# One forget-bias tile per head, a re-priced task order, and three PSUM banks for scores beside two for projections

## The chip, the core and the metric

The kernel runs on one core of a Trainium2 chip. The metric is the time of one execution in device microseconds (us); lower is better. Engines are named as the profile names them: PE (TensorE matmul) with PEld (its weight loads), DVE (VectorE), ACT (ScalarE), POOL (GpSimd), SP (SyncE, which issues the DMAs). Each engine runs its own list of instructions in order, and waits at an instruction whose inputs or buffers are not there.

## The reference

One layer of a hybrid attention encoder over two requests that share weights: a prompt of 1040 rows (16 meta tokens and 1024 frames) and a sample of 32 rows with a cache of 272 rows. The input is normalised, projected, and split into a differential attention group (4 heads of two maps, bias by distance, mask by chunks of 64) and a forgetting attention group (8 heads of 64, causal). The forgetting group's bias is the part that the change touches:

```python
logf = jax.nn.log_sigmoid((fl + b_f_l).astype(jnp.float32))
F = jnp.cumsum(LF, axis=1)
...
sf = jnp.einsum('bqhe,bkhe->bhqk', qf, Kf).astype(f32) * scale
sf = sf + (Fq_t[:, :, :, None] - Fk_t[:, :, None, :])
sf = jnp.where(kidx[None, :] <= qidx[:, None], sf, NEG)
pf = jax.nn.softmax(sf, axis=-1)
of = jnp.einsum('bhqk,bkhe->bqhe', pf.astype(Vf.dtype), Vf)
```

Since a softmax over k does not change when a number that depends on q alone is added, the bias of a key may be F at any reference point minus F of that key. The heads' outputs are multiplied by silu(gate), projected with w_out, added to the input and normalised:

```python
y = x + (out.astype(x.dtype) * jax.nn.silu(gate)) @ w_out_l
...
y_prompt = _rmsnorm(hp[:, N_META:], final_norm_g)
```

The new rows of k, v and log f are outputs too.

## The kernel before

The program first builds a graph of tasks, and `Graph.order` (line 149) simulates it: each task (`add`, line 100) names an engine, a cost in ns, a priority (a smaller number goes first), the tasks it depends on, the buffers it takes (`acq`) and uses (`use`). At each moment a free engine starts its ready task of smallest priority for which buffers are free. The order in which tasks start in this simulation is the order in which their instructions are written, one after the other, to every engine. So the costs are no computation of the kernel; they settle the order alone. The costs are formulas (`c_mm`, `c_act`, `c_dve`, `c_ts`, `c_pool`, lines 266 to 279, with `MARGIN` 1.1) or numbers at the place, a change of engine costs one of `HOPS` (line 33), and a DMA's landing follows from lines 203 to 209: SP is busy for `cost`, the bytes go one transfer after the other at 2.85 ns per KB, 0.9 us later they are there, and 8 may be in flight. A task of an output tile that will be ready within `AHEAD` ns holds back later ones.

Buffers come from rings (`RINGS`, line 247). The plan counts the free ones of a ring. The tile that a task gets in the program is the ring's next in turn. PSUM has 8 banks: pj 3 (projections and the output projection), sc 2 (scores, and small work of the sample), tr 1 (transposes, and the spread of a scale), av 2 (attention times values). Other memory is taken from one `arena`.

The work, in pairs p of heads or maps (p 0 to 3 differential, p 4 to 7 forgetting, two heads each):

- `x_tasks` (line 471) normalises x and writes it transposed, in f16 high and low parts, as hT.
- `w_tasks` (611) loads 128 columns of a weight, finds its largest value (ACT L627; `spread_task`, line 575: POOL L583 makes a diagonal, PE L587 spreads it into tr, DVE L600 takes the maximum) and splits it in high and low parts.
- `proj_tasks` (796) does a projection (kinds v, k, q, g for the gate) in three groups of columns, four for v and k of pair 0. Each group takes one pj bank and writes 24 matmuls (L827) in three parts of 8, between which other work may go. Its readers: for k and v ACT L845; for q ACT L889 and DVE L894, and in the last group L905 and L910; for the gate ACT L920 (exp), then DVE L924, ACT L928 and L929, DVE or POOL L933, DVE L937, and DVE L938, which reads the bank last.
- `forget_tasks` (979) computes log f and its running sum F for 8 heads. Lines 1106 to 1116 subtract F at four columns, one per group of 256 queries (DVE L1113), and store the results as four sections of `G_s`.
- `bias_tasks` (1148) makes the bias tile of 128 x 1040 in the ring G of two. For p below 4 it is made once per pair. For p of 4 and more the first call loads the pair's rows of G_s, scales them (POOL L1180) and stores them in `G_t`; every call then loads one section's first 272 + 256 gg columns, broadcast over 128 partitions (SP L1192), for one head and one group gg.
- `unit_tasks` (1206) does two blocks of 128 queries: scores (PE L1235 and, for the causal mask, L1237) in chunks of at most 512 keys, each in one sc bank; DVE L1249 adds the bias, takes the minimum and writes to the arena; ACT L1255 the exponential with its sum; DVE L1259 and L1261 the reciprocal; split in high and low f16 parts on ACT, POOL and DVE (L1284 to L1323); SP L1335 transposes by DMA; PE L1347 to L1354 multiply with the values into av. `fin_tasks` writes the result to mix_s in DRAM.
- `sample_tasks` (1448) does the same for the 32 sample rows.
- `out_tasks` (1607) splits w_out, and for nine row tiles loads mix and gate, multiplies them (L1723), finds the scale (ACT L1737 and a spread), splits (ACT L1740, DVE L1742), multiplies with w_out (L1770, two halves, each with a pj bank), adds x (L1784), squares (L1789), normalises (L1808) and stores (L1811).

`pair_tasks` (1843) calls these for a pair. For p of 4 and more its units go in the order (head 0, gg 0), (head 1, gg 0), (head 0, gg 1) and so on, eight in all, each with a bias tile of its own:

```python
for u, (hd, gg) in enumerate(units):
    if p >= 4 or u == 0:
        dist = bias_tasks(p, hd, gg, base + u - 1, G_done)
```

The projections of later pairs and the gate (priorities from 10000) fill TensorE between the units.

## Time and profile before

| | us |
|---|---|
| median of 3 runs (lowest, highest) | 882.83 (881.67, 883.38) |
| profiled execution, its time | 879.12 |
| its span, first to last instruction | 877.4 |
| mean granted clock of TensorE | 0.909 of full speed |

A row of the waits reads "engine line waited for: us in total, times, longest us"; PE av L1351 <- DMA arena<-arena is a matmul of line 1351 into av that waited for a DMA from arena to arena, here the transpose. A row of the groups of instructions reads: line, engine, operation, what it writes and reads, shapes, count, then busy us and mean ns of one, then the idle time of the engine just before them with what ended it. In the table of windows each engine has its busy us and its instructions (x), followed by the granted clock (1.00 is full), the busy share of the DMA engines and GB/s. In the timeline a row has its start and length in us; in brackets stands the idle time before it and what ended it.

### The profile page before, as it was taken

The numbers are of one execution on the slowest core, as the hardware profiler recorded it, in microseconds if no ns is written. First come the engines' busy times: TensorE is split into PE (matmuls) and PEld (weight loads), VectorE is DVE, ScalarE is ACT, GpSimd is POOL, SyncE is SP. The second block draws the span as 40 slices with busy tenths as digits, with TensorE's granted clock in tenths as the row PEclk, the third lists the DMA queues.
The fourth block names the chain that finished last, engine by engine and source line by source line (L and its number), as shares of the span: only waits on it lengthen the run. The fifth ranks groups of instructions, "written<-read, shape, count | busy, mean of one in ns | idle before, by whom it ended". The sixth has DMA issues, their size and how long they took to land. (4 is left out here: it accounts for less than half of the span.)

```text
span 877.4 us, 14974 instructions
## 1 busy us (share of the span) xinstructions
PE 703.1 (80%) x4967; PEld 456.3 (52%) x4967; DVE 633.0 (72%) x1672; ACT 496.5 (57%) x1136; POOL 414.3 (47%) x602
## 2 busy tenths in 40 slices
PE   4578887987876999899796978689788962888776
PEld 4455554665544576566564755356556542233333
DVE  5976587877766887988985857497797895454443
ACT  5843574666553776676675665377568752242222
POOL 2575233977556866866743654445452244200000
PEclk7679989999998999999998989799999985698899
DMA  8672426454423554554499688467959989753511
GB/s 248 122 147 62 93 54 88 106 94 103 95 65 74 127 102 98 115 117 115 105 194 182 127 168 163 111 144 167 208 123 204 277 204 243 232 173 121 153 63 49
DMA packets 240558, 119.27 MB, mean 136 GB/s; under 512 B 150569, under 2 KB 229745, under 8 KB 240481
## 3 DMA queue, kind: packets, MB, share of 16 engines
q1 hardware_dynamic: 240480, 118.32, 60.4%
q8 instruction: 39, 0.64, 0.3%
q14 instruction: 39, 0.31, 0.1%
HBM read 57.18 MB, written 22.07 MB: 90 GB/s over the span
## 5 line engine op out<-in xcount | busy, mean ns | idle before, releaser
L827 PE MATMUL pj<-hT,Whi 128*128 128x384 f16 (+4 forms) x1328 | 314.7, 321 | 2.0 <-DVE ge L938 1.5
L827 PE MATMUL pj<-hT,Wlo 128*128 128x416 f16 (+4 forms) x664 | 212.6, 320 | 4.4 <-DVE Wlo L648 4.4
L827 PEld LDWEIGHTS <-Whi 128*128 128x128 f16 x1328 | 133.3, 102 | 78.5 <-issue 11.5
L1249 DVE CUSTOM_DVE_ANT_0 arena<-sc,G,stats 128x400 f32<-128x400 f32 (+6 forms) x224 | 129.9, 590 | 43.3 <-PE sc L1235 22.4
L1255 ACT ACTIVATE arena<-arena,stats 128x144 f32<-128x144 f32 (+7 forms) x128 | 99.9, 780 | 38.8 <-DVE stats L1249 31.6
L1235 PE MATMUL sc<-k,q 128*128 128x400 f16 (+6 forms) x448 | 97.1, 317 | 29.4 <-DVE stats L1249 25.7
L583 POOL TENSOR_SCALAR diag<-ident,stats 128x128 bf16<-128x128 f32 x51 | 26.1, 513 | 154.9 <-ACT Wlo L1737 68.5
L827 PEld LDWEIGHTS <-Wlo 128*128 128x128 f16 x664 | 67.6, 102 | 38.1 <-DVE Wlo L648 4.7
L1351 PE MATMUL av<-arena,vn 128*128 128x128 f16 x288 | 43.9, 236 | 45.2 <-DMA arena<-arena 44.7
L1235 PEld LDWEIGHTS <-q 128*128 128x128 f16 x448 | 40.8, 101 | 57.6 <-issue 41.1
L627 ACT ACTIVATE Wlo<-raw 128x1024 bf16<-128x1024 f32 x27 | 28.5, 1055 | 63.8 <-DMA raw<-in_w_in_dram 63.8
L1770 PEld LDWEIGHTS <-Whi 128*128 128x128 f16 (+2 forms) x304 | 30.1, 102 | 58.7 <-issue 16.5
L827 PE MATMUL pj<-hT,Wghi 128*128 128x256 f16 (+2 forms) x240 | 58.2, 326 | 0.0
L1770 PE MATMUL pj<-arena,Whi 128*128 128x512 f16 (+4 forms) x152 | 49.7, 413 | 9.8 <-ACT Whi L1740 7.1
L1352 PEld LDWEIGHTS <-vn 128*128 128x128 f16 x288 | 30.7, 107 | 48.6 <-issue 47.6
L1290 POOL TENSOR_TENSOR arena<-arena 128x16 f16<-128x16 f32 (+7 forms) x56 | 46.5, 853 | 12.4 <-ACT arena L1284 12.1
L1306 DVE SCALAR_TENSOR_TENSOR arena<-arena,stats 128x128 f16<-128x128 f32 (+4 forms) x80 | 49.6, 663 | 2.6 <-ACT arena L1298 2.4
L1323 POOL TENSOR_TENSOR arena<-arena 128x16 f16<-128x16 f32 (+3 forms) x48 | 36.0, 773 | 25.8 <-ACT arena L1317 25.7
L1789 ACT ACTIVATE arena<-arena 128x512 bf16<-128x512 f32 (+3 forms) x19 | 11.5, 603 | 61.4 <-DVE arena L1784 61.4
L1352 PE MATMUL av<-arena,vn 128*128 128x128 f16 x288 | 44.3, 237 | 0.0
L1784 DVE SCALAR_TENSOR_TENSOR arena<-pj,stats,arena 128x512 f32<-128x512 f32 (+3 forms) x19 | 13.7, 721 | 42.3 <-PE pj L1770 38.9
L587 PE MATMUL tr<-diag,onesb 128*128 128x128 bf16 x51 | 11.7, 229 | 36.9 <-POOL diag L583 24.6
(310 smaller groups left out, 1786.7 us busy)
## 6 DMA issues: line engine op xcount, KB each, us to landing
raw<-in_w_in_dram SPq DMA_DIRECT2D x32, 512.0 KB, 7.5
arena<-in_x_prompt_dram SPq DMA_DIRECT2D x16, 512.0 KB, 9.7
raw<-in_w_out_dram SPq DMA_DIRECT2D x16, 512.0 KB, 4.6
k<-k SPq DMA_DIRECT2D x16, 268.0 KB, 3.4
G<-G_t SPq DMA_DIRECT2D x8, 520.0 KB, 4.7
mix_s<-mx SPq DMA_DIRECT2D x32, 128.0 KB, 3.4
arena<-mix_s SPq DMA_DIRECT2D x8, 512.0 KB, 6.3
arena<-gate_s SPq DMA_DIRECT2D x8, 512.0 KB, 6.0
```

The source lines that it names most:

```text
L583: pool.tensor_scalar(out=loc["d"], in0=ident, scalar1=col_, scalar2=1.0, op0=ALU.mult, op1=ALU.mult)
L627: ta = add("act", c_act(1024), lambda: act.activation(out=loc["lo"].bitcast(BF16), in_=loc["raw"], func=AF.Abs, accum_out=a), prio, [tl], ...
L827: mm(out, (W["hi"], W["hi"], W["lo"])[w][:, k, :], (hTh, hTl, hTh)[w][:, k, c0:c1], start=i == 0, stop=i == 23)
L1235: mm(s[:, :b - a], q, K[p]["t"][:, m, x, a:b], start=x == 0, stop=x == 1 and not mask)
L1249: dve.tensor_tensor_reduce(out=A(ph, nk)[:, a:b], in0=loc["s"][:, :b - a], in1=bl["t"][:, o + a:o + b], scale=Q[p]["tau"], scalar=3e38 if ...
L1255: te = add("act", c_act(nk) + 150, lambda ph=ph, nk=nk, mn=mn, sm=sm: act.activation(out=A(ph, nk), in_=A(ph, nk), func=AF.Exp, scale=-1.0 ...
L1290: (pool if on_pool else dve).tensor_tensor(out=A16(w, o, o + b - a), in0=x[:, a:b], in1=A16(w, h, h + b - a), op=ALU.subtract)
L1306: dve.scalar_tensor_tensor(out=A16(w, o, o + b - a), in0=x[:, a:b], scalar=rk, in1=A16(w, h, h + b - a), op0=ALU.mult, op1=ALU.subtract)
L1323: pool.tensor_tensor(out=A16(w, o, o + b - a), in0=x[:, a:b], in1=A16(w, h, h + b - a), op=ALU.subtract)
L1351: mm(out, vn[:, j, 128 * hd:128 * hd + 128], hi, start=j == 0, stop=False)
L1352: mm(out, vn[:, j, 128 * hd:128 * hd + 128], lw, start=False, stop=False)
L1770: mm(d, a, b, start=k == 0 and i == 0, stop=k == 7 and i == len(ops) - 1)
```

## The change

Three things are changed at once; the arithmetic of scores and outputs is otherwise the same.

1. One forget-bias tile per head. F is taken relative to column 528 alone; G_s and G_t have 1040 columns per head in place of 4160; a pair loads and scales two rows; a head's tile of 1040 columns is loaded once per pair and used for all four groups of queries.
2. Costs of the planner. Formulas and numbers at the place are replaced; a hop's cost depends on the producing engine; TensorE is charged twice the cost after 3.4 us of idleness, for 3.4 us; a DMA transpose (`block`) holds the DMA queue in the plan; a ring's buffers are taken in turn in the plan too, as they are in the program.
3. PSUM: pj 2 and sc 3.

In `out_tasks` a part of the matmuls names the two pieces of w_out that it reads in place of all eight.

```diff
-HOPS = [400.0, 300.0], [500.0, 300.0]
+HOPS = {"pe": 220.0, "sp": 100.0, "act": 80.0, "dve": 80.0, "pool": 80.0}
+SLACK = {"pe": 0.0, "act": 0.0, "dve": 0.0, "pool": 0.0, "sp": 0.0}
+COLD = 3400.0
+TRANSPOSED = 2000.0
+LANDED = 1600.0
...
-MARGIN = 1.1
...
-                if self.free[h.ring] < 1:
+                if self.slots[h.ring][self.turn[h.ring]]:
                     break
-                self.free[h.ring] -= 1
+                h.at = self.turn[h.ring]
+                self.slots[h.ring][h.at] = True
+                self.turn[h.ring] = (h.at + 1) % self.free[h.ring]
...
-                        busy[e] = now + t.cost
+                        cost = t.cost
+                        if e == "pe":
+                            if now > last + COLD:
+                                slow = COLD
+                            cost += min(cost, slow)
+                            slow = max(0.0, slow - cost + t.cost)
+                            last = now + cost
+                        busy[e] = now + cost
                         done = busy[e]
-                        if e == "sp":
-                            moved = max(done + 650.0, moved) + t.move
-                            done = moved + 900.0
-                            flight = (flight + [done] * t.n)[-8:]
-                            if len(flight) == 8:
-                                busy[e] = max(busy[e], flight[0])
+                        if t.dma:
+                            if t.block:
+                                busy[e] = done = moved = max(now, moved - 300.0) + t.cost
+                                done += TRANSPOSED
+                            else:
+                                busy[e] = max(busy[e], moved - 4000.0)
+                                moved = max(busy[e] + 300.0, moved) + t.move
+                                done = moved + LANDED
...
-    RINGS = {"pj": 3, "sc": 2, "tr": 1, "av": 2, "stv": 1, "raw": 2, "W": 3, "Wg": 2, "zT": 2, "stg": 2, "vn": 2, "K": 2,
+    RINGS = {"pj": 2, "sc": 3, "tr": 1, "av": 2, "stv": 1, "raw": 2, "W": 3, "Wg": 2, "zT": 2, "stg": 2, "vn": 2, "K": 2,
...
-        return k * max(107.0, 0.417 * n)
+        return k * max(56.0, 2.5 + 0.417 * n)
...
-        return MARGIN * k * (75.0 + 0.84 * n)
+        return k * (165.0 + 0.85 * n)
...
-        return MARGIN * k * (65.0 + 1.05 * n)
+        return k * (165.0 + 1.08 * n)
...
-        return MARGIN * (100.0 + 1.1 * n)
+        return 240.0 + 1.05 * n
...
-        return MARGIN * k * (100.0 + 2.2 * n)
-
-    def dma(fn, prio, deps=(), acq=(), use=(), kb=128, n=1, spare=(), cost=480.0):
-        t = add("sp", cost * n, fn, prio, deps, acq, use, 2.85 * kb, spare)
+        return k * (160.0 + 2.2 * n)
+
+    def dma(fn, prio, deps=(), acq=(), use=(), kb=128, n=1, spare=(), cost=440.0, move=4.5, block=False):
+        t = add("sp", cost * n, fn, prio, deps, acq, use, move * kb, spare)
...
-        td = add("pool", 260, fd, prio, list(deps) + [cn["id"]], [dh])
-        return loc, th, add("pe", 110, f, prio, [td, cn["one"]], [th], [dh])
+        td = add("pool", 370, fd, prio, list(deps) + [cn["id"]], [dh])
+        return loc, th, add("pe", 60, f, prio, [td, cn["one"]], [th], [dh])
...
+        def fg():
+            F = A(Fh, 1040, NH)
+            dve.tensor_scalar(out=A(gh, 1040, NH), in0=F, scalar1=F[:, 528:529], scalar2=None, op0=ALU.subtract)
+        tg = add("dve", 65 + 0.6 * 1040, fg, prio, carry, [gh], [Fh])
+        G_done["p"] = dma(lambda: sp.dma_start(out=G_s, in_=A(gh, 1040, NH)), prio, [tg], [], [gh])
...
-        n = 272 + 256 * gg
-        if ("G", p) not in samp:
+        if hd == 0:
...
+        c = 2 * (p - 4) + hd
 
         def f():
             loc["t"] = T([128, 1040], F32, "G", RINGS["G"])
-            c = 1040 * (4 * hd + gg)
-            sp.dma_start(out=loc["t"][:, :n], in_=G_t.rearrange("h n -> (h n)")[None, 8320 * (p - 4) + c:8320 * (p - 4) + c + n]
-                         .broadcast_to([128, n]))
-        cn["bias"] = dma(f, prio, [samp["G", p], cn["bias"]], [h], kb=n / 2)
+            sp.dma_start(out=loc["t"], in_=G_t[c:c + 1].broadcast_to([128, 1040]))
+        cn["bias"] = dma(f, prio, [samp["G", p], cn["bias"]], [h], kb=520)
...
-                     prio, [tl], [z], [w], kb=20 * nt, cost=1190.0)
+                     prio, [tl], [z], [w], kb=20 * nt, cost=1100.0 + 40.0 * nt, block=True)
...
-                             [ph] if part == 0 else [], [wh] + wholds + ([ph] if part else []))
+                             [ph] if part == 0 else [], [wh] + wholds[2 * part:2 * part + 2] + ([ph] if part else []))
...
-        dist = None
+        dist = {}
         for u, (hd, gg) in enumerate(units):
-            if p >= 4 or u == 0:
-                dist = bias_tasks(p, hd, gg, base + u - 1, G_done)
+            if hd not in dist:
+                dist[hd] = bias_tasks(p, hd, base + u - 1, G_done)
...
-            unit_tasks(p, hd, gg, base + u, dist, av)
+            unit_tasks(p, hd, gg, base + u, dist[hd], av)
```

Some forty more numbers at the place change in the same manner, most of them upwards: the two-part scaling of v on POOL from 1500 to 3000, the transposes of x from 1190 to 2640 with `block`, a weight's load from 2.85 to 10 ns per KB.

More of the change, by code (lines that the diff above doesn't have):

```diff
@@ L96, in __init__ @@
         self.free = dict(rings)
+        self.slots = {r: [False] * n for r, n in rings.items()}
+        self.turn = dict.fromkeys(rings, 0)
         self.arena = arena
@@ L137, in _take @@
         ok = len(got) == len(t.acq) + len(spare)
-        for h in got[len(t.acq):] if ok else got:
+        for h in got[len(t.acq):] if ok else got[::-1]:
             self._give(h)
+            if h.ring != "arena":
+                self.turn[h.ring] = h.at
         return ok
@@ L146, in _give @@
         else:
-            self.free[h.ring] += 1
+            self.slots[h.ring][h.at] = False
     def order(self):
@@ L161, in order @@
         n = 0
-        now = moved = 0.0
-        flight = []
+        now = 0.0
+        last = slow = 0.0
+        moved = 0.0
         while events or later:
@@ L176, in order @@
                     d.wait -= 1
-                    d.ready = max(d.ready, now + (0.0 if d.eng == t.eng else HOPS[d.eng == "pe"][d.prio > 10400]))
+                    d.ready = max(d.ready, now + (0.0 if d.eng == t.eng else HOPS[t.eng] + SLACK[d.eng]))
                     if d.wait == 0:
@@ L305, in tile_hymba @@
     gate_s = dr.tile([1024, NT], F32, tag="gate_s", name="gate_s")
-    G_s = dr.tile([NH, 4 * 1040], F32, tag="G_s", name="G_s")
-    G_t = dr.tile([NH, 4 * 1040], F32, tag="G_t", name="G_t")
+    G_s = dr.tile([NH, 1040], F32, tag="G_s", name="G_s")
+    G_t = dr.tile([NH, 1040], F32, tag="G_t", name="G_t")
     Gs_s = dr.tile([NH, LS], F32, tag="Gs_s", name="Gs_s")
@@ L456, in f2 @@
                 dve.scalar_tensor_tensor(out=r, in0=r0, scalar=by[0][:n], in1=t, op0=ALU.mult, op1=ALU.mult)
-        t1 = add("act", cost + 330, f1, prio, deps, [], use)
-        return r, t1, add("dve", 530, f2, prio, [t1, by and by[1]])
+        t1 = add("act", cost + 420, f1, prio, deps, [], use)
+        return r, t1, add("dve", 1170, f2, prio, [t1, by and by[1]])
     hT_ready = {}
@@ L625, in fl @@
             sp.dma_start(out=loc["raw"], in_=wi[:, :, c:c + 128])
-        tl = dma(fl, prio, [], [rh, wh], kb=512)
+        tl = dma(fl, prio, [], [rh, wh], kb=512, move=10.0)
         ta = add("act", c_act(1024), lambda: act.activation(
@@ L740, in fw @@
             pool.tensor_copy(out=v["new"], in_=v["st"][:32, 9])
-        v["t_new"] = add("pool", 550, fw, prio, ts, [nh], [sh])
+        v["t_new"] = add("pool", 340, fw, prio, ts, [nh], [sh])
         v["nh"] = nh
@@ L964, in fq @@
                     pool.tensor_copy(out=qz[2][o:o + 64, 32 * m:32 * m + 32], in_=q[o:o + 64])
-            Q[p]["z"] = add("pool", 950, fq, prio, [Q[p]["sample"], cn["c"], samp.get(("score", p - 1))], [], [Q[p]["qh"]])
+            Q[p]["z"] = add("pool", 870, fq, prio, [Q[p]["sample"], cn["c"], samp.get(("score", p - 1))], [], [Q[p]["qh"]])
             inv, tau = stat(), stat()
@@ L973, in proj_tasks @@
             Q[p]["tau"], Q[p]["inv"] = tau, inv
-            Q[p]["t_tau"] = add("dve", 470, ft, EV(prio), [tw, K[p]["tw"]])
+            Q[p]["t_tau"] = add("dve", 900, ft, EV(prio), [tw, K[p]["tw"]])
     samp = {}
@@ L998, in fw @@
             loc["raw"] = raw
-        tw = add("pool", 400, fw, prio, [ts, cn["gs"]], [zh], [wh])
+        tw = add("pool", 2500, fw, prio, [ts, cn["gs"]], [zh], [wh])
         tw = add("dve", 140, lambda: dve.scalar_tensor_tensor(
@@ L1105, in forget_tasks @@
         G_done = {}
-        for gg in range(4):
-            n = 1040
-            gh = Hold("arena", n)
-            def fg(gg=gg, n=n, gh=gh):
-                F = A(Fh, 1040, NH)
-                b = 16 + 256 * gg
-                dve.tensor_scalar(out=A(gh, n, NH), in0=F[:, :n], scalar1=F[:, b:b + 1], scalar2=None, op0=ALU.subtract)
-            tg = add("dve", 65 + 0.6 * n, fg, prio, carry, [gh], [Fh])
-            G_done[gg] = dma(lambda gg=gg, n=n, gh=gh: sp.dma_start(
-                out=G_s[:, 1040 * gg:1040 * gg + n], in_=A(gh, n, NH)), prio, [tg], [], [gh])
+        gh = Hold("arena", 1040)
+        def fg():
[3 more added lines that the diff above has]
+        G_done["p"] = dma(lambda: sp.dma_start(out=G_s, in_=A(gh, 1040, NH)), prio, [tg], [], [gh])
         ph, FSh, GSh = Hold("pj"), Hold("arena", LS), Hold("arena", LS)
@@ L1425, in f3 @@
             act.activation(out=r0, in_=r0, func=AF.Exp, scale=-0.5)
-        t3 = add("act", c_act(n, 2), f3, prio, [t2], [], [fh, sh])
+        t3 = add("act", c_act(n, 2) + 60, f3, prio, [t2], [], [fh, sh])
         def f4():
@@ L1557, in ft @@
             s["pt"] = t
-        tt = add("pe", 500, ft, prio, [tn, cn["c"]], [th_], [Ph])
+        tt = add("pe", 760, ft, prio, [tn, cn["c"]], [th_], [Ph])
         def fh():
@@ L1793, in out_tasks @@
                              [xh] + ([jh] if half else []))
-                    ts0 = add("dve", 70, lambda ss=ss, half=half: dve.tensor_scalar(
+                    ts0 = add("dve", 160, lambda ss=ss, half=half: dve.tensor_scalar(
                         out=ss[half], in0=ss[half], scalar1=1.0 / 1024.0, scalar2=ss[half - 1] if half else 1e-6,
```

72 lines of the change are left out of this document (38 added, 34 removed).

## The prediction

> **What bounds the kernel now.** I read the busy shares first, then the table of windows, which cuts the span into the stage that prepares x and the first weights (0 to 60), the body of projections and attention (60 to 720), the hand-over (720 to 746) and the output projection (746 to the end). The columns after each engine are its busy us; then come the granted clock, the share of the DMA engines and GB/s.
>
> ```profile
> span 877.4 us, 14974 instructions
> ...
> PE 703.1 (80%) x4967; PEld 456.3 (52%) x4967; DVE 633.0 (72%) x1672; ACT 496.5 (57%) x1136; POOL 414.3 (47%) x602
> ```
>
> ```profile
> 0.00:60.00 60.00, 32.98 (x220) 27.33 (x221) 47.81 (x82) 37.04 (x69) 29.17 (x24) 0.72 0.75 172
> 60.00:720.00 660.00, 555.99 (x4236) 378.51 (x4235) 508.42 (x1430) 416.80 (x975) 365.04 (x559) 0.95 0.62 130
> 720.00:746.00 26.00, 7.72 (x65) 6.81 (x64) 16.47 (x28) 5.56 (x12) 11.37 (x9) 0.50 0.98 232
> 746.00:878.00 132.00, 106.40 (x448) 43.68 (x448) 60.34 (x134) 37.13 (x83) 8.73 (x12) 0.87 0.41 131
> ```
>
> TensorE is the fullest engine in every stage but the first and third, and it never saturates: it idles 27 us, 104 us (660 - 556), 18 us and 26 us in the four stages, 175 in all. The body is where most of it lies. VectorE is busy 77% there (508 of 660), so two engines share the work with neither at its limit: what costs time is that each, running its instructions in one fixed order, stands before one that isn't ready. The waits of TensorE and of VectorE within the body say before which.
>
> ```profile
> PE av L1351 <- DMA arena<-arena: 33.5, 17, 8.7
> PE sc L1235 <- DVE stats L1249: 25.7, 29, 3.0
> PE tr L587 <- POOL diag L583: 13.9, 6, 4.5
> PE tr L587 <- ACT stg L712: 8.7, 3, 5.9
> ...
> PE pj L827 <- DVE ge L938: 1.5, 1, 1.5
> ```
>
> ```profile
> DVE arena L1249 <- PE sc L1235: 22.4, 20, 4.8
> ...
> DVE arena L1249 <- PE sc L1237: 13.3, 15, 4.3
> ```
>
> Columns: us in total, times, longest. Four rows of TensorE hold 82 of its 104 us. Probabilities that come back late from the transposing DMA: 33.5. Score matmuls that wait for VectorE to leave one of the two score banks (sc): 25.7. The one bank for the scale spread (tr): 22.6. For a projection bank (pj) of the three it waited once, 1.5 us. And VectorE in turn stood 35.7 us before a score that TensorE had not written: both sides wait for each other over two banks.
>
> **The change part by part.** The sum is made against the profiled execution's own 879.12 us (span 877.4); the median of the runs is 882.83, 3.7 above, and I add that at the end.
>
> *A, the third score bank (sc 2 to 3).* With three banks TensorE writes score k+2 while VectorE reads k, if the order lets it. It can take away 25.7 us of TensorE's idle time at most and nothing at least; VectorE's 35.7 us shrink with it but are the same moments seen from the other side, so they are not added. A wait averages 0.9 us (25.7 / 29), and the next row has one reduction at 0.59: one more bank covers one reduction, which is most of an average wait, but the longest, 3.0, it does not. Part of what is won TensorE will lose before the next unready instruction. I take half: **-13**, bounds 0 and -26.
>
> ```profile
> L1249 DVE CUSTOM_DVE_ANT_0 arena<-sc,G,stats 128x400 f32<-128x400 f32 (+6 forms) x224 | 129.9, 590 | 43.3 <-PE sc L1235 22.4
> ...
> L583 POOL TENSOR_SCALAR diag<-ident,stats 128x128 bf16<-128x128 f32 x51 | 26.1, 513 | 154.9 <-ACT Wlo L1737 68.5
> ```
>
> *B, one bias tile per head.* Removed: 24 of 32 loads from G_t, three stores to G_s, three L1113 subtractions. What remains is 8 loads of 520 KB.
>
> ```profile
> G<-G_t SPq DMA_DIRECT2D x8, 520.0 KB, 4.7
> ...
> G<-G_t SPq DMA_DIRECT2D x8, 392.0 KB, 4.3
> ...
> G<-G_t SPq DMA_DIRECT2D x8, 264.0 KB, 6.2
> ...
> arena<-arena SPq DMA_TRANSPOSE x96, 4.5
> ...
> G<-G_t SPq DMA_DIRECT2D x8, 136.0 KB, 3.4
> ```
>
> ```profile
> SPq L1192 <- DVE stats L1249: 9.5, 9, 4.1
> ```
>
> Bytes: 8 x (520 + 392 + 264 + 136) = 10,496 KB become 4,160, so 6.3 MB go, all in the last two thirds of the body, where the forget heads run. In the hand-over row the DMA engines, 98% busy with the same mixture, moved 232 GB/s; at that rate 6.3 MB are 27 us of all engines. The Trainium skill's page "DMA: Bandwidth & Descriptors", section Specifications, gives 435 GB/s as the fabric's ceiling; by it the same bytes would be an estimated 14.6 us. The trace's rate, about half the ceiling, decides, as it contains the short packets of the transposes. SyncE issues in order, and it stood 9.5 us before such a load whose G slot was still being read, with transposes queued behind it; inside a pair these waits go, since the tile stays. Who benefits is L1351: 33.5 us behind transposes. The forget heads are where it waits, but a transpose also waits for its own producers on POOL and DVE, which don't change. I take a third: **-11**, bounds 0 and -33. Against it stands that the first unit of a pair needed 136 KB (3.4 us to landing) and now needs 520 KB (4.7 us): 1.3 us at four pairs, two heads, at most 10 us in all; the slot is free as early as before (a ring of two; the seventh unit of a pair releases it), and the eighth unit's scores and the projections cover the landing, so I count nothing, and 10 us if they don't. The scale of G in POOL (L1180) has 2 rows in place of 8 at the same length, and costs the same. The three L1113 (745 ns each by a row shown with D, 2.2 us in all) lie in the forget preparation beside projections: nothing.
>
> *C, the order from other durations.* No instruction changes its length; the planner does. It priced the spread's POOL step at 260 ns where the row above says 513 (now 370), and let a ring's next user take any free bank where the buffers really go round in turn (now they do in the plan too). So the plan should put fewer instructions ahead of something that is not ready. What it reaches apart from A and B is the tr row, 22.6 us, with one bank as before. Without a row of the new order the gain can lie anywhere from none to 22.6, and a greedy order can also come out worse by as much. I take a fifth, since one price of this row is half mended: **-4**, bounds -23 and +23.
>
> *D, two projection banks (pj 3 to 2).* This part costs. A bank is held from the first of 24 matmuls to its last reader. Here is one gate group of 384 columns: a matmul that begins it and its last one, its first reader and its last.
>
> ```profile
> 572.04 0.49 PE L827 MATMUL pj<-hT,Wghi 128*128 128x384 f16 x2
> ...
> 576.54 0.33 PE L827 MATMUL pj<-hT,Wglo 128*128 128x384 f16 x1
> ```
>
> ```profile
> 576.99 0.58 ACT L920 ACTIVATE ge<-pj,stats 128x384 f32<-128x384 f32 x1
> ```
>
> ```profile
> 586.23 0.62 DVE L938 SCALAR_TENSOR_TENSOR ge<-pj,stats,gr 128x384 f32<-128x384 f32 x1
> ```
>
> Filling took 4.8 us, draining another 10.0 (576.87 to 586.85). With three banks two more groups could be filled meanwhile; with two, one. There are 98 groups (50 of k and v, by the row below, 24 of q, 24 of the gate) in 660 us, one per 6.7 us; two banks give one per 7.4 us if every group were held 14.8, but k and v groups have a single short reader of 0.45 us, and they are half of all.
>
> ```profile
> L845 ACT ACTIVATE zT<-pj 128x416 f32<-128x416 f32 (+4 forms) x50 | 22.3, 447 | 21.7 <-PE pj L827 19.0 <-PE tr L587 2.4
> ...
> L1113 DVE TENSOR_SCALAR arena<-arena 8x1040 f32<-8x1040 f32 x4 | 2.8, 745 | 0.1
> ```
>
>  So on average there is room, and where gate and query groups follow each other there is not. The score and av matmuls can run in the gap if they are ready. Bounds: nothing (all gaps filled), and 40 us (20 of the 48 gate and query groups making the next wait 2 us). I take what 9 such waits of 1 us cost, near the row of today's 1.5 us for one: **+9**.
>
> *E, the output projection and the start.* The tail's gaps come from a rule that stays: TensorE takes the matmuls of one row tile before the spread of the next, so this spread stands behind them.
>
> ```profile
> 806.12 0.37 POOL L583 TENSOR_SCALAR diag<-ident,stats 128x128 bf16<-128x128 f32 x1 [15.30 <-ACT Wlo L1737]
> ```
>
> ```profile
> 816.25 0.23 PE L587 MATMUL tr<-diag,onesb 128*128 128x128 bf16 x1 [0.99 <-DVE stats L600]
> 818.41 1.03 PE L1770 MATMUL pj<-arena,Whi 128*128 128x512 f16 x2 [1.93 <-ACT Whi L1740]
> 820.91 0.61 PE L1770 MATMUL pj<-arena,Wlo 128*128 128x512 f16 x1 [1.47 <-DVE Wlo L1742]
> ```
>
> The spread's input was ready at 806.5, TensorE ran it at 816.25, and then chains through VectorE and ScalarE until 820.9: about 4.4 us of idle (0.99 + 1.93 + 1.47), at three places. Priorities of the row tiles are the same, and two pj banks suffice there: a half's reader L1784 follows at once while the other half is filled. Nothing, with 8 us either way.
>
> **Sum:** 879.1 - 13 - 11 - 4 + 9 + 0 = 860.1 by the profiled execution; with 3.7 for the median **863.8 us**, 2.2% faster.
>
> **The rivals.** *The projection banks decide (slower).* Place: gate and query groups side by side, L827 waiting for L938, L894 or L910. For it: 14.8 us per gate group, and groups begun as filler and interrupted hold a bank still longer. Against: today there is one such wait. At its bound of 40 us it gives 879.1 - 28 + 40 = 891, 895 as a median. It decides from 28 us on, the sum of A, B and C.
>
> *The waits only move.* TensorE stops standing before one instruction and stands before the next, because VectorE with 508 us of work and the chain score, reduction, exponential, transposition, av set the pace. For it: the two engines' waits mirror each other; against: neither is over 85% busy in the body. A, B, C and D then cancel: 879, a median of 883.
>
> *More goes than I count.* Waits caused by one wrong plan have one cure. If A gives 20, B 22 and C 11 and D costs 9, it is 879.1 - 44 = 835, a median of 839. For it: all four rows are waits for things the old plan mispriced; against: the same plan must now live with two projection banks.
>
> **How the numbers follow.** The forecast with its own range 850 to 876 gets 0.46, the larger gain 0.20, waits that move 0.10, the banks 0.24. A measurement of this kernel can tell about 0.2% (1.8 us) from no change. Faster by more than that: 0.46 + 0.20 + 0.02 of the moved waits = 0.68; within it 0.08; slower 0.24. The range reaches to 834 (the larger gain and 5 us of the tail) and to 892 (just short of the banks' bound): about a tenth is left out on each side.
>
> **What would show it.** A is right if L1235's wait for L1249 falls from 25.7 to 13 or less; B if 8 loads from G_t are left, SyncE's waits before them are near zero and L1351's wait is about 22; C if the two L587 rows shrink; D if L827 waits for L938, L894 or L910 some 9 us in all. E is right if the output projection, from 746 to the end before, again takes about 131 us. The prediction is wrong if L827's waits pass 28 us, if the body isn't shorter although the four rows shrink (then a new wait has taken their place), or if the stage before 60 or after 720 moves by more than 8 us.

## The result, and the profile after

The changed kernel takes **827.18 us** (median; 825.07 to 830.70), the kernel before 883.11 in the same comparison: a ratio of 0.937 [0.933, 0.941], 6.3% faster. The forecast was 863.8 us, 2.2% faster, with a range down to 834; the direction was right and the size was not.

The page of the changed kernel opens with these lines (span, then busy us, share of the span and instructions):

```profile
span 829.0 us, 14876 instructions
...
PE 696.9 (84%) x4967; PEld 454.7 (55%) x4967; DVE 632.0 (76%) x1669; ACT 495.4 (60%) x1136; POOL 421.1 (51%) x602
```

The span is 48.4 us shorter. TensorE's busy time is 6.2 us shorter, its idle time 42.2 (877.4 - 703.1 = 174.3 before, 829.0 - 696.9 = 132.1 now). The other engines do the same work as before. The table of windows shows in which stage; the stages now end where attention ends, at 682 and before at 738.3. First the changed kernel, then the one before, cut in the same way:

```profile
60.00:682.00 622.00, 556.59 (x4330) 384.76 (x4329) 521.17 (x1449) 423.16 (x987) 388.62 (x568) 0.96 0.65 133
682.00:718.00 36.00, 16.71 (x35) 3.66 (x35) 19.40 (x29) 7.10 (x12) 8.89 (x10) 0.59 0.91 267
718.00:829.00 111.00, 90.67 (x414) 40.38 (x413) 49.82 (x117) 31.89 (x76) 3.47 (x7) 0.93 0.30 96
```

```profile
60.00:738.30 678.30, 563.45 (x4300) 385.32 (x4299) 518.82 (x1447) 420.66 (x982) 373.38 (x564) 0.94 0.63 132
738.30:759.00 20.70, 10.67 (x28) 2.57 (x28) 11.39 (x19) 5.14 (x9) 5.99 (x7) 0.65 1.09 320
759.00:878.00 119.00, 95.99 (x422) 41.11 (x422) 55.02 (x125) 33.69 (x78) 5.78 (x8) 0.89 0.34 107
```

The body became 56 us shorter, 49 of it idle time (678.3 - 563.45 = 115 before, 65 now). The end, from the last matmul with values on, became 8 us longer (139 to 147). So the gain lies in the body, and most of it in waits. TensorE's there, in the changed kernel (lines moved by 22 to 27: L827 is now L854, L1235 L1257, L1249 L1271, L587 L614, L1351 L1373):

```profile
PE av L1373 <- DMA arena<-arena: 15.4, 8, 4.0
PE sc L1257 <- DVE stats L1271: 11.5, 15, 4.1
PE tr L614 <- POOL diag L610: 7.8, 9, 1.4
PE pj L854 <- DVE ge L965: 7.5, 7, 3.3
PE pj L854 <- ACT zT L872: 3.4, 1, 3.4
PE av L1369 <- DMA arena<-arena: 3.4, 3, 1.4
PE pj L854 <- DVE q L921: 2.3, 1, 2.3
```

In the kernel before, with the body cut in the same way, the first row is larger than in the prediction, whose window ended at 720:

```profile
PE av L1351 <- DMA arena<-arena: 44.7, 21, 8.7
```

All four rows that the prediction named have shrunk; they hold 93 us before on this cut (the other three are as in the prediction), and 35 after. The waits for projection banks are there, 13.2 us in three rows. The largest change of all is in a row that the prediction doesn't name. These are ScalarE's waits of the kernel before, from the table of waits of all engines, where the first is third from the top:

```profile
ACT Wlo L627 <- DMA raw<-in_w_in_dram: 63.8, 21, 8.2
...
ACT Wglo L627 <- DMA raw<-in_w_in_dram: 18.4, 3, 8.8
```

ScalarE stood 82 us before weights that had not landed, and behind that instruction stood, in its list, the exponentials and the copies out of projection banks. In the changed kernel the first row is down to a third (the second to 2.0):

```profile
ACT Wlo L654 <- DMA raw<-in_w_in_dram: 19.4, 7, 6.4
```

### The profile page after: what moved, and what is told of

Read it like the earlier page. It is cut to its first block, busy times and chain, and to the rows that moved or that the text cites. A ratio compares the mean times of both kernels' runs of the same rounds, so it can differ in the third digit from the quotient of the medians.

```text
span 829.0 us, 14876 instructions
## 1 busy us (share of the span) xinstructions
PE 696.9 (84%) x4967; PEld 454.7 (55%) x4967; DVE 632.0 (76%) x1669; ACT 495.4 (60%) x1136; POOL 421.1 (51%) x602
## 5 line engine op out<-in xcount | busy, mean ns | idle before, releaser
L854 PE MATMUL pj<-hT,Whi 128*128 128x416 f16 (+4 forms) x1328 | 313.4, 321 | 13.5 <-DVE ge L965 6.7
L854 PE MATMUL pj<-hT,Wlo 128*128 128x416 f16 (+4 forms) x664 | 212.4, 321 | 0.0
L854 PEld LDWEIGHTS <-Whi 128*128 128x128 f16 x1328 | 132.5, 101 | 90.4 <-issue 22.9
L1271 DVE CUSTOM_DVE_ANT_0 arena<-sc,G,stats 128x400 f32<-128x400 f32 (+9 forms) x224 | 128.6, 588 | 13.0 <-PE sc L1257 3.8
L1277 ACT ACTIVATE arena<-arena,stats 128x656 f32<-128x656 f32 (+7 forms) x128 | 99.9, 781 | 31.4 <-DVE stats L1271 30.9
L1257 PE MATMUL sc<-k,q 128*128 128x400 f16 (+9 forms) x448 | 91.0, 313 | 13.7 <-DVE stats L1271 11.5
L854 PEld LDWEIGHTS <-Wlo 128*128 128x128 f16 x664 | 67.4, 102 | 34.4 <-issue 2.2
L1792 PEld LDWEIGHTS <-Whi 128*128 128x128 f16 (+2 forms) x304 | 30.3, 102 | 69.7 <-issue 27.2
L1257 PEld LDWEIGHTS <-q 128*128 128x128 f16 x448 | 40.3, 100 | 35.8 <-issue 19.1
L854 PE MATMUL pj<-hT,Wghi 128*128 128x256 f16 (+2 forms) x240 | 57.1, 324 | 0.8 <-DVE ge L965 0.8
L1373 PE MATMUL av<-arena,vn 128*128 128x128 f16 x288 | 42.7, 233 | 16.0 <-DMA arena<-arena 15.4
L1345 POOL TENSOR_TENSOR arena<-arena 128x16 f16<-128x16 f32 (+3 forms) x48 | 37.9, 812 | 22.1 <-ACT arena L1339 22.0
L1312 POOL TENSOR_TENSOR arena<-arena 128x16 f16<-128x16 f32 (+7 forms) x56 | 44.3, 815 | 1.9 <-ACT arena L1306 1.8
L1374 PE MATMUL av<-arena,vn 128*128 128x128 f16 x288 | 42.9, 233 | 0.0
L1811 ACT ACTIVATE arena<-arena 128x512 bf16<-128x512 f32 (+3 forms) x19 | 11.5, 603 | 49.6 <-DVE arena L1806 49.6
L654 ACT ACTIVATE Wlo<-raw 128x1024 bf16<-128x1024 f32 x27 | 28.3, 1048 | 19.6 <-DMA raw<-in_w_in_dram 19.4
L854 PE MATMUL pj<-hT,Wglo 128*128 128x256 f16 (+2 forms) x120 | 38.7, 322 | 1.4 <-DVE Wglo L675 1.4
```

The lines of the kernel that those rows point to most:

```text
L654: ta = add("act", c_act(1024), lambda: act.activation(out=loc["lo"].bitcast(BF16), in_=loc["raw"], func=AF.Abs, accum_out=a), prio, [tl], ...
L854: mm(out, (W["hi"], W["hi"], W["lo"])[w][:, k, :], (hTh, hTl, hTh)[w][:, k, c0:c1], start=i == 0, stop=i == 23)
L1257: mm(s[:, :b - a], q, K[p]["t"][:, m, x, a:b], start=x == 0, stop=x == 1 and not mask)
L1271: dve.tensor_tensor_reduce(out=A(ph, nk)[:, a:b], in0=loc["s"][:, :b - a], in1=bl["t"][:, o + a:o + b], scale=Q[p]["tau"], scalar=3e38 if ...
L1277: te = add("act", c_act(nk) + 125, lambda ph=ph, nk=nk, mn=mn, sm=sm: act.activation(out=A(ph, nk), in_=A(ph, nk), func=AF.Exp, scale=-1.0 ...
L1312: (pool if on_pool else dve).tensor_tensor(out=A16(w, o, o + b - a), in0=x[:, a:b], in1=A16(w, h, h + b - a), op=ALU.subtract)
```

## The experiments

For each run the table has the median, the ratio to the kernel before of the same comparison with its 95% interval, and from the profiled execution: the length of attention (from the first reduction of scores with their bias, L1249 or L1271, to the last matmul with values), TensorE's idle time in it, and the time from there to the end; then, over the whole span, TensorE's waits behind transposes, its waits of L1235 (L1257) for the reduction, and ScalarE's waits for weights (both L627 or L654 rows). All in us.

| run | median | ratio | attention | idle in it | end | transposes | score bank | weights |
|---|---|---|---|---|---|---|---|---|
| before | 883.1 | 1 | 645 | 111 | 139 | 46 | 26 | 82 |
| the change | 827.2 | 0.937 [0.933, 0.941] | 576 | 59 | 147 | 19 | 12 | 21 |
| only_order | 893.1 | 1.012 [1.006, 1.017] | 651 | 110 | 136 | 23 | 40 | 26 |
| only_bias | 875.7 | 0.994 [0.990, 0.997] | 641 | 105 | 136 | 51 | 18 | 84 |
| only_psum | 893.7 | 1.013 [1.009, 1.017] | 624 | 117 | 169 | 39 | 9 | 89 |
| bias_psum | 856.8 | 0.972 [0.968, 0.977] | 600 | 98 | 153 | 33 | 15 | 81 |
| order_bias | 858.9 | 0.974 [0.971, 0.977] | 606 | 76 | 147 | 20 | 31 | 19 |
| order_bias_n | 851.0 | 0.966 [0.962, 0.970] | 598 | 74 | 148 | 24 | 32 | 17 |
| order_psum | 871.0 | 0.988 [0.985, 0.991] | 639 | 97 | 125 | 22 | 17 | 21 |
| order_psum_n | 866.8 | 0.983 [0.979, 0.987] | 625 | 91 | 135 | 40 | 12 | 15 |
| before_m112 | 895.9 | 1.016 [1.012, 1.021] | 662 | 117 | 138 | 46 | 30 | 79 |
| after_j1 | 845.5 | 0.961 [0.956, 0.965] | 584 | 71 | 153 | 22 | 5 | 20 |
| plan_held | 885.3 | 1.006 [1.003, 1.008] | 642 | 106 | 137 | 33 | 22 | 19 |
| dead_loads | 859.6 | 0.975 [0.971, 0.979] | 594 | 73 | 156 | 20 | 17 | 20 |
| old_dma_model | 891.9 | 1.012 [1.006, 1.017] | 632 | 107 | 159 | 24 | 6 | 106 |
| w_price_off | 852.1 | 0.966 [0.960, 0.971] | 597 | 80 | 158 | 19 | 11 | 66 |
| w_price_off_n | 867.9 | 0.985 [0.979, 0.991] | 606 | 81 | 159 | 26 | 10 | 60 |
| w_price_old | 851.1 | 0.966 [0.961, 0.972] | 614 | 90 | 137 | 41 | 29 | 22 |
| w_price_old_n | 857.0 | 0.974 [0.970, 0.979] | 622 | 96 | 133 | 38 | 33 | 23 |
| tail_early | 807.4 | 0.917 [0.912, 0.922] | 575 | 60 | 129 | 22 | 10 | 21 |

**Each part alone.** *only_order* is the changed kernel with the old bias tiles and the old banks; *only_bias* the kernel before with one tile per head; *only_psum* the kernel before with the new banks:

```diff
-    RINGS = {"pj": 3, "sc": 2, "tr": 1, "av": 2, "stv": 1, "raw": 2, "W": 3, "Wg": 2, "zT": 2, "stg": 2, "vn": 2, "K": 2,
+    RINGS = {"pj": 2, "sc": 3, "tr": 1, "av": 2, "stv": 1, "raw": 2, "W": 3, "Wg": 2, "zT": 2, "stg": 2, "vn": 2, "K": 2,
```

> The planner's new costs, hops, DMA model and ring turns alone; 32 bias loads and pj 3, sc 2 as before. If the order makes the gain (theory 1), 835 to 850 us, and the waits behind transposes (44.7 us before, 15.4 after) and before the scale spread (22.6 before, 8.4 after, within the attention) both shrink to within 10 us of the changed kernel's. If the bias tile makes it (theory 2), the waits behind transposes stay above 35 us and the time is 865 to 875. If the third score bank makes it (theory 3), L1249's release still costs the scores over 20 us and the time is 865 to 875.

> One bias tile per head alone, with the old planner and the old banks. Theory 1 (the order): 875 to 885 us, and the waits behind transposes stay above 35 us. Theory 2 (the bias tile): 850 to 862, and these waits fall below 20 us, since 24 loads with 6.3 MB and SyncE's 9.5 us of waits before them are gone. Theory 3 (the score bank): 875 to 885.

> pj 2 and sc 3 alone, with the old planner and 32 bias loads. Theories 1 and 2: 875 to 895 us, since 14 us of the scores' waits go and as much comes in waits for a projection bank. Theory 3 (the score bank makes the gain): 850 to 865. If the two projection banks need a plan that knows the turn of the ring, L827's waits for its readers are 15 us or more here.

Measured: 1.2% slower, 0.6% faster, 1.3% slower. None has the gain, and their effects (by the ratios +10, -6 and +11 us on 883) add up to about +16 where the change has -56. The last two came out as expected of parts that don't make the gain alone; 893.1 for the new planner lies outside every range given for it. Each does what it says to its own row: the new planner takes ScalarE's weights from 82 to 26 and the transposes from 46 to 23, three banks take the score bank's row from 26 to 9. But the time comes back elsewhere: with the new planner and two score banks that row is 40; with the new banks and the old planner the end is 30 us longer.

**Two parts at a time.** *bias_psum* is the kernel before with the tile and the banks; *order_bias* and *order_psum* are the changed kernel with the old banks, and with the old tiles.

> Bias tile and banks together, the old planner. Theory 1 (the order): 870 to 890 us. If bias tile and score bank make the gain together, without the order: 835 to 850.

> The new planner and one bias tile per head, but pj 3 and sc 2 as before. If the banks matter (theory 3 in part), 840 to 855 us, with the scores' wait for L1249's release back above 20 us; if the order alone makes the gain (theory 1), within 5 us of the changed kernel's 827.

> The new planner and the new banks, but 32 bias loads. If the bias tile matters (theory 2 in part), 840 to 855 us with the waits behind transposes above 25 us; if not, within 5 us of 827.

Measured: 856.8, 858.9, 871.0. Any two of the parts give 1 to 3%, where one alone gives less than 1% or loses. None of the three times lies in a range that was expected of it; the score bank's row is back above 20 us in order_bias, as expected, and the waits behind transposes are not above 25 in order_psum. With these, all eight combinations of the three parts have run. Added last, the tile is worth 44 us (871.0 to 827.2), the banks 32 (from 858.9) and the planner 30 (from 856.8); added first they are worth 6, -11 and -10. Each of these is a difference between two single plans.

**How much is luck of a plan?** The order is found greedily, so a price moved by one or two per cent gives another order of the same kind. *after_j1* does that to the changed kernel, *before_m112* to the one before, and the runs ending in *_n* to their namesakes (with the first of these edits, but for w_price_old_n, which has a margin of 1.09):

```diff
-        return k * (165.0 + 1.08 * n)
+        return k * (168.0 + 1.10 * n)
```

```diff
-MARGIN = 1.1
+MARGIN = 1.12
```

> The changed kernel with one formula of the planner nudged: VectorE's cost from 165 + 1.08 n to 168 + 1.10 n ns, under 2%. Nothing is computed otherwise; it shows how far a greedy order moves the time by chance. If chance is small against the gain, 820 to 836 us; if the 827 is a lucky draw, 840 or more.

> The kernel before with the planner's MARGIN at 1.12 in place of 1.1: the same nudge for the old plan. If chance is small, 874 to 892 us; if the old plan's 883 is an unlucky draw, 865 or less.

> The new planner and banks with 32 bias loads again, with VectorE's cost nudged to 168 + 1.10 n as in the nudged changed kernel (845.5 us). If the bias tile's effect is not chance, it is 860 us or more; if it is chance, 855 or less.

> The changed kernel with the old banks (two for scores, three for projections), and its price of VectorE's work moved by 2% so that another plan of the same kind comes out. The first such plan took 858.9 with waits for a score bank of 47.0 us. If the third score bank is worth some 14 to 30 us in the full change, whatever the plan's luck, this one takes 850 to 870 and waits over 40 us for score banks. If the 859 was an unlucky plan, this one takes less than 848.

Measured: 845.5 where the change has 827.2, as was expected if 827 is a lucky draw, and 895.9, just above its range, where before has 883.1; the other pairs differ by 7.9 (order_bias), 4.2 (order_psum), 5.8 and 15.8 us (the weight runs below). So up to 18 us between two single plans says nothing of a cause, and the changed kernel's own 827 may hold as much of it: a neighbouring plan has a gain of 3.9% in place of 6.3%. The rows of the score bank and of the weights hold better than the times. The row behind transposes doesn't always: it is 22 us in order_psum and 40 in its neighbour. Without the third bank the body's score row stands in both plans, here in order_bias_n,

```profile
PE sc L1257 <- DVE stats L1271: 31.6, 28, 7.0
```

against 11.5 with it (5.3 in after_j1): 19 to 26 us of TensorE's waiting. The times with and without it differ by 31.7 in one pair of plans and 5.5 in the other.

**Is the bias tile's gain the bytes?** *dead_loads* is the changed kernel that also issues the 24 removed loads (6.3 MB), into arena space that no one reads, at the place in the plan where they used to be:

```diff
+                dead = dead_load(p, hd, gg, u, base, [samp["G", p], red[(p, *units[u - 2])], dead if u > 2 else None])
...
+        return dma(lambda: sp.dma_start(out=A(dh, n), in_=G_t[c:c + 1, 0:n].broadcast_to([128, n])), base + u - 1, deps,
+                   [dh], [], kb=n / 2)
```

*plan_held* issues nothing more. Only the plan is told that a unit waits for a load of that size, which in turn waits for the unit two before it, as it was with a ring of two tiles:

```diff
+                held = dma(lambda: None, base + u - 1, [red[(p, *units[u - 2])], held if u > 2 else bias[2]],
+                           kb=(272 + 256 * gg) / 2)
+                bias = (bias[0], bias[1], held)
```

> The changed kernel with 24 further loads that nothing reads: for the third to eighth unit of each forget pair 272, 272, 528, 528, 784 and 784 columns of G_t go to a scratch buffer, after the reductions of the unit two before, at the old loads' priority. So the 6.3 MB and SyncE's issues are back, but no unit waits for them. If the bias tile helps by its bytes and issues (theory 2a): 855 to 875 us, and more wait behind transposes than 18.8 us by at least 10. If it helps because the units are no longer tied to a load and to the unit two before (theory 2b): 820 to 850, the scatter of a nudged plan.

> The changed kernel, 8 loads and no more, but planned as if each unit from the third on of a forget pair waited for a load that itself waits for the reductions of the unit two before: an empty task of the load's cost stands in the plan and issues nothing. Theory 2a (bytes and issues): 820 to 850 us. Theory 2b (the tie between units in the plan): 855 to 880, near the 871 of the new planner and banks with 32 loads, with over 85 us of TensorE idle in the attention stage (59 us in the changed kernel, 97 with 32 loads).

Measured: 859.6 with the loads, 885.3 with the tie alone, the latter 5 us above the range given for the tie. The loads cost 14 to 32 us (against 845.5 and 827.2; much of it may be the plan's luck), the tie, which moves no byte, 40 to 58. That is no less than the tile is worth in the change and in its neighbour (44 and 21 us). TensorE's waits in the body, dead_loads first, then plan_held:

```profile
PE pj L854 <- DVE ge L965: 16.9, 9, 3.9
PE sc L1258 <- DVE stats L1272: 16.8, 25, 2.6
PE av L1374 <- DMA arena<-arena: 16.1, 10, 6.5
```

```profile
PE av L1374 <- DMA arena<-arena: 27.7, 17, 7.5
PE sc L1258 <- DVE stats L1272: 21.5, 20, 4.8
PE tr L614 <- POOL diag L610: 11.8, 10, 3.9
PE sc L1548 <- POOL qz L989: 10.5, 7, 5.9
```

The time of dead_loads is the one expected if the bytes count, its row is not: with 6.3 MB more the wait behind transposes is 16.1 us, against 15.4 without, where 10 more were expected. With the tie it is 27.7, the score row 21.5 in spite of three banks, and idle time in attention goes from 59 to 106 us. The reading is that the tile brings above all that any unit may come when its inputs are there. This rests on one plan, but one that lies well outside the 18 us. The tie is not quite alone in it: the plan of plan_held also keeps transfer time for loads that never come (8 x (264 + 392 + 520) = 9,408 KB). dead_loads keeps such time too, for 6,336 KB, and moves the bytes, and is 26 us faster; the 3 MB by which the two plans differ are not separated from the tie.

**Which price of the new planner?** *old_dma_model* is the changed kernel with the old model of transfers in the planner (2.85 ns per KB, 8 in flight, transposes like other loads). *w_price_off* changes one number of the changed kernel, *w_price_old* one number of the kernel before (1796 x 2.85 ns is the same 5.1 us):

```diff
-        tl = dma(fl, prio, [], [rh, wh], kb=512, move=10.0)
+        tl = dma(fl, prio, [], [rh, wh], kb=512)
```

```diff
-        tl = dma(fl, prio, [], [rh, wh], kb=512)
+        tl = dma(fl, prio, [], [rh, wh], kb=1796)
```

> The changed kernel with the old planner's model of a DMA (2.85 ns per KB, eight in flight, a transpose priced as any other) and everything else new. If pricing transposes is what brought the waits behind them down from 46.5 to 18.8 us, they are 33 us or more here and the time is 840 to 865 us; if it is another part of the new plan, they stay below 25 and the time is 820 to 850.

> The changed kernel, except that the planner charges a weight load of 512 KB like any other load (4.5 ns per KB, about 2.3 us) instead of 10 ns per KB (5.1 us). Theory 1: this one price is what moved the weight loads forward; ScalarE then again stands over 50 us before weights that have not landed (before: 63.8 + 18.4; changed: 19.4 + 2.0), TensorE's waits for the scale spread go back above 45 us, and the time is 845 to 880. Rival: the transposes' price (block of the queue, 2.6 and 1.1 us and more) is what counts; ScalarE's wait stays below 30 us and the time is 820 to 845, the scatter that a price moved by 1% or 2% made of plans.

> The kernel before, except that its planner charges a weight load about 5.1 us of the transfer queue instead of 1.5 us; all else, one bias tile per unit, two score banks and three projection banks, stays. If the weight price alone brings the loads forward, ScalarE's wait for weights falls from 82 (63.8 + 18.4) to below 30 us and the time to 850 to 870. If the old planner's other prices and its free choice of a ring's slot spoil it, the wait stays above 45 us or another takes its place, and the time is 875 to 895.

> The kernel before with the weight load priced at 5.1 us, as in the run that took 851.1, and the planner's margin on ScalarE's and VectorE's work 1.09 in place of 1.10, so that another plan of the same kind comes out. If the price of the weight load is worth about 30 us by itself, this one takes 840 to 868 and ScalarE stands below 30 us before weights; if the 851 was a lucky plan, it takes 870 to 900.

> The changed kernel with the weight load at the common price, as in the run that took 852.1, and the small shift of VectorE's price that by itself took the changed kernel from 827 to 845.5. If the weight price matters in the new planner too, ScalarE stands over 45 us before weights and the time is 850 to 880. If the other prices are enough there, ScalarE may stand as long but the time is 825 to 848.

Measured: 891.9; 852.1 and 867.9; 851.1 and 857.0. With the old model of transfers the whole gain is gone, outside both expected ranges. ScalarE stands 106 us before weights there, since that price is the old one too; the row behind transposes is 24 us, so the price of a transpose isn't what keeps it short. The four weight runs lie in the ranges expected if this price matters. Taken out of the changed kernel the one price costs 24.9 and, in the neighbouring plans, 22.3 us (867.9 - 845.5). Put alone into the kernel before it gains 3.4% [2.8, 3.9] and 2.5% [2.1, 3.0], more than any of the three parts alone. The rows say what it does. In w_price_old ScalarE's wait, over the span, and TensorE's largest, in the body:

```profile
ACT Wlo L627 <- DMA raw<-in_w_in_dram: 17.7, 8, 4.6
```

```profile
PE av L1351 <- DMA arena<-arena: 35.5, 21, 5.1
PE sc L1235 <- DVE stats L1249: 28.8, 28, 4.9
PE av L1347 <- DMA arena<-arena: 5.5, 4, 2.4
PE sc L1416 <- DVE stats L1249: 5.4, 4, 3.2
PE sc L1235 <- DVE sX L1598: 3.1, 1, 3.1
PE pj L827 <- DVE ge L938: 1.7, 3, 0.8
PE sc L1578 <- DVE stats L1259: 1.6, 1, 1.6
```

The transposes and the score bank are where they were; the two L587 rows (22.6 us before) are gone from a list that goes down to 1.6. And w_price_off brings the first of them back, with ScalarE's wait above it:

```profile
ACT Wlo L654 <- DMA raw<-in_w_in_dram: 54.1, 19, 7.5
```

```profile
PE tr L614 <- POOL diag L610: 20.8, 9, 5.5
```

So the row of the spread is fed from further up: weight load, largest value on ScalarE, diagonal on POOL, spread on TensorE. In the kernel before, the load landed 7.5 us after its issue (the median of six loads, 5.7 to 11.8). Its plan had it land after 3.5 us on a free queue (0.48 of SyncE, 0.65, 512 x 2.85 ns = 1.46 of transfer, 0.9) and so put its reader too early; the new plan has it land after 7.5 (0.44, 0.3, 5.12 and 1.6), as long as the measured median. In the Trainium skill, the page "DMA: Bandwidth & Descriptors", section Specifications, has 435 GB/s as the ceiling, an estimated 1.2 us for these bytes. The old plan's 1.46 us was near that; a landing among other transfers took far longer, and the landing is what the reader waits for.

This price is also most of what the planner is worth. With the tile and the new banks, the old planner takes 856.8 (bias_psum), the new one with the common price in its place 852.1, and with it 827.2: 25 of the 30 us are this one number, and the other 5 are less than the plans scatter. With the old tiles and the old banks, the old planner with this price takes 851.1 and 857.0 (w_price_old and its neighbour) and the whole new planner 893.1 (only_order), with ScalarE's wait short in all three (22, 23 and 26 us): there the rest of the new planner costs 36 to 42 us, about twice what single plans scatter. The old planner with this price, the tile and the banks together was not run.

**The gaps of the end.** *tail_early* gives a row tile's preparation in the output projection (product, largest value, spread, split) a priority 15 lower, so that the next tile's spread goes ahead of this tile's matmuls:

```diff
             pr = prio + 10 * t
+            pe_ = pr - 15
...
-            ta = add("act", c_act(8 * n), fa, pr, [t1], [wh], [rh])
-            sc, ts = scale_tasks(a, pr, [ta], [(1.0, uo, u)])
+            ta = add("act", c_act(8 * n), fa, pe_, [t1], [wh], [rh])
+            sc, ts = scale_tasks(a, pe_, [ta], [(1.0, uo, u)])
```

> The changed kernel, except that in the output projection the preparation of a row tile (its product with the gate, the largest value, its spread and the scale, the split into two halves) gets a priority 15 lower, so that the plan places the spread of the next row tile ahead of this one's matmuls. If the gaps of about 5 us between row tiles come from that rule, TensorE's idle time in the tail falls from 39.8 to below 28 us, the tail from 147 to about 135 us, and the time is 810 to 822. If the gaps come from elsewhere (gate values or inputs late, the arena full), the tail stays within 5 us of 147 and the time is 822 to 850.

Measured: **807.43 us**, 0.917 [0.912, 0.922], the best of all, 2.2% less than the change (0.917 over 0.937). Attention is as it was (575, idle 60); the end went from 147 to 129, TensorE's idle time in it from 39.8 to 26.5. One boundary of the changed kernel, in TensorE's timeline:

```profile
740.67 0.22 PE L614 MATMUL tr<-diag,onesb 128*128 128x128 bf16 x1
741.88 0.23 PE L614 MATMUL tr<-diag,onesb 128*128 128x128 bf16 x1 [0.99 <-DVE stats L627]
744.04 0.61 PE L1792 MATMUL pj<-arena,Whi 128*128 128x512 f16 x2 [1.93 <-ACT Whi L1762]
746.28 0.61 PE L1792 MATMUL pj<-arena,Wlo 128*128 128x512 f16 x1 [1.64 <-DVE Wlo L1764]
746.68 1.06 PE L1792 MATMUL pj<-arena,Whi 128*128 128x512 f16 x2
747.53 0.63 PE L1792 MATMUL pj<-arena,Wlo 128*128 128x512 f16 x1
...
749.11 0.60 PE L1792 MATMUL pj<-arena,Whi 128*128 128x512 f16 x2
749.54 0.38 PE L1792 MATMUL pj<-arena,Wlo 128*128 128x512 f16 x1
...
767.88 0.22 PE L614 MATMUL tr<-diag,onesb 128*128 128x128 bf16 x1
769.09 0.23 PE L614 MATMUL tr<-diag,onesb 128*128 128x128 bf16 x1 [0.99 <-DVE stats L627]
```

and one of tail_early, where the spread passes between two matmuls and nothing waits:

```profile
730.38 0.22 PE L614 MATMUL tr<-diag,onesb 128*128 128x128 bf16 x1
730.44 0.59 PE L1793 MATMUL pj<-arena,Whi 128*128 128x512 f16 x2
...
740.80 0.22 PE L614 MATMUL tr<-diag,onesb 128*128 128x128 bf16 x1
...
751.21 0.22 PE L614 MATMUL tr<-diag,onesb 128*128 128x128 bf16 x1
```

In the changed kernel the spreads come in twos (740.67 and 741.88, then 767.88 and 769.09), so two row tiles take 27.2 us (767.88 - 740.67); in tail_early the spreads come one by one, and two tiles take 20.8 (751.21 - 730.38). Three such places make 19 us.

## Why the prediction was right and wrong

**Where it failed: C, the order from other durations.** It was taken as -4 with bounds of 23, on the ground that "one price of this row is half mended", that of the diagonal on POOL (260 to 370). The two L587 rows fell from 22.6 to 8.6 us, 14 where 4 was forecast. The row was right, its owner was not. The prediction read the 22.6 us as waits for the one tr bank, but 13.9 of them are waits for the diagonal, an input. These rows hang on the weight loads, whose price went from 1.46 to 5.1 us in the same change; that price stands in the list of changes and has no term in the sum. It is worth 22 to 25 us in the changed kernel and 22 to 30 in the kernel before (2.5 and 3.4% of 883). The part of the working that led astray is "the waits of TensorE and of VectorE within the body say before which": ScalarE's 82 us stood near the top of the table of waits.

Read from the rows on the same cut of the body, the terms are A -14 us (forecast -13), the transposes -28 with both of their rows (46.5 to 18.8; forecast -11), the spread -14 (-4) and the projection banks +12 (+9): -44 in place of -19, where the idle time fell by 49. So the transposes and the spread are the two that were sized too small.

**B, one bias tile.** Forecast -11, from bytes. Size and mechanism are both off. "8 loads left" came true, none of SyncE's larger waits is before them any more, and the row behind transposes fell to 15.4, further than the 22 forecast. But it falls with the planner in plans with the old tiles too (22.5 over the span in only_order, against 44.7), though not in all of them (40 with both rows in order_psum_n), and not with the tile alone under the old planner (35.8 and 14.8 in two rows of only_bias). Beside the other two parts the tile is worth 44 us, or 21 in the neighbouring plans (871.0 and 866.8 against 827.2 and 845.5); with no other part it is worth 6. By plan_held most of it is the tie to a load and to the unit two before it, which the prediction had only as 9.5 us of SyncE's waiting.

**A, the third score bank.** Right in the row: 25.7 to 11.5, -14 where -13 was forecast, and the row is at 40 us with the new planner and two banks (only_order), at 9 with the old planner and three (only_psum). What it is worth in time is not settled beyond the row's 19 to 26 us, since the pairs give 5.5 and 31.7.

**D, two projection banks.** Right: 13.2 us of waits for L965, L872 and L921 where there was 1.5; +9 was forecast. The rival in which these banks decide needed 28.

**E, start and end.** At its edge: the end is 8 us longer. Its gaps were named with their cause and left at nothing, as the rule stays; tail_early shows the cause was right. The hand-over is 15 us longer (36 us in place of 21, at a clock of 0.59) and the rest of the end 8 us shorter (111 in place of 119). In the hand-over, matmuls of the output projection stood 5.0 and 4.5 us before pieces of w_out that VectorE was still splitting (L1712); what would help there was not tried.

**The sum.** Adding the parts assumed that each one's row falls alone. Shown is that they don't add: about +16 for the three alone, -56 together. The rival "more goes than I count" (839), with "one wrong plan" behind all the rows, was nearer than the forecast. That the three parts free each other's waits is the reading of the rows; it is seen for the score bank and the new planner, where ScalarE's wait for weights goes and the score bank's row rises to 40 us until the third bank is there. What in the new planner shortens the waits behind transposes stays open: the weight price put into the old planner leaves them at 41 over the span, taking it out of the new one at 19, and the old transfer model at 24. That leaves among others the prices of the engines, the hops and the turns of the rings.

## What to carry to other kernels

Where an order is planned from costs, compare the plan's price of every transfer with its measured landing before anything else, and read the waits of all engines: the engine that stood first in the chain here, ScalarE, was busy for 57% of the span. Parts that share one plan must be measured together, and a plan moved by a per cent of a price shows how far a single time may be trusted. A gap that comes back in a regular stage can cost more than its idle time: here 6.4 us for 4.6 us of idling.

## What the runs showed of the hardware

After the stalls of the end TensorE runs at half pace for a while. In the boundary shown above two matmuls of 512 columns take 0.85 us from 746.68 to the next start, at 749.11 only 0.43; the granted clock is 0.50 from 746.2 to 747.5 and 1.00 from 749.1 on. The same comes back at the other two boundaries, and in tail_early, where the gaps are gone, the clock is 1.00 from 730 to 800. Of the 6.4 us that a boundary costs, 4.6 are idle (0.99 + 1.93 + 1.64), and 1.3 are the half pace: seven matmuls take 2.83 us from 746.28 to 749.11, and would take 1.51 at the later pace. Here no single gap was longer than 1.93 us; three of them within 5.4 us, with three matmuls between, came before each drop of the clock. The rule of the new planner, twice the cost after 3.4 us of idleness, would charge nothing for such gaps. The Trainium skill, page "TensorE: Matmul & The Clock Gate", Part 1, has the array go to half rate after an idle window of about 3.4 us. Here shorter gaps that follow each other closely were enough.
